# A row-wise softmax in 12 tiles instead of 11: five rows first, nine and six last, and a first store that no longer waits for the third load

## The chip, the core and the metric

The kernel runs on one core of one Trainium2 chip. The core has 16 DMA engines that move data between its on-chip memory (SBUF, 128 partitions) and device memory (HBM), and compute engines that each follow their own queue of instructions. Here four of those queues matter: VectorE (DVE), ScalarE (ACT), GpSimd (POOL) and SyncE (SP). SP, POOL and ACT also issue the transfers. The metric is the time of one execution in microseconds on the device; lower is better. Before the change the median of three runs is 317.19 us (317.1 to 317.5).

## The reference

A softmax over the last axis of a float32 array of 32 x 512 x 1024, after a division by a temperature of 0.5:

```python
def reference(x, temperature):
    scaled = x / temperature
    shifted = scaled - np.max(scaled, axis=-1, keepdims=True)
    exp_x = np.exp(shifted)
    return (exp_x / np.sum(exp_x, axis=-1, keepdims=True)).astype(np.float32)
```

That is 16,384 rows of 1,024 elements, 4 KB each: 67.11 MB are read and as many written, and every element is touched by one maximum, one exponential with a sum, and one multiplication.

## The kernel before

The 16,384 rows are cut into tiles. A tile has 128 partitions, and each partition holds k consecutive rows of the input, so a "tile of twelve rows" is 128 x 12 rows and 6,144 KB. The list `PASSES` (line 10) names the tiles and, inside each tile, the groups of rows that are computed together: one tile of 4+4+4 rows, nine of 6+6 and one of 4+4, 128 rows per partition in all, 11 tiles and 23 groups.

The pool of tiles has four buffers of twelve rows (`BUFS`, line 11). All arithmetic is in place: a tile is loaded, normalised where it lies, and stored from there. The four first loads are issued at once on SP's queue. After that `load()` (line 56) is called once after each store, so the load of tile i+4 stands behind the landing of the store of tile i, whose buffer it takes. SP issues all loads in order.

For each group g there are four steps. `maximum(g)` is one DVE reduction over the group (line 69) and a small DVE multiplication that makes the bias (line 72). `exponential(g)` is one ACT instruction for each row, with the row's sum accumulated beside it (line 78). `divide(g)` takes a reciprocal on DVE (line 90) and multiplies: in tiles listed in `WHOLE` with one tensor-by-tensor multiplication for the whole group (line 93), in the others with one tensor-by-scalar multiplication per row (line 96). `store(g)` issues the store of the whole tile once its last group has been divided (line 108), on POOL's queue for tiles before number `BY_POOL`, on ACT's for the others.

The order on every engine is written out by hand (`manual_schedule`). In a step of the loop, the maximum and exponential of group g come first, and then the division of group g-1, so DVE can reduce the next group while ACT works on the one before. It follows that the store of tile i stands on DVE behind the first reduction of tile i+1, and so behind the landing of load i+1. From tile `ALONE` on the order is turned round at the first group of a tile: the former tile is divided and stored before the next one is reduced.

Ahead of the first store POOL copies one element of tile 2 (line 106). The copy does no work for the result; it makes POOL wait until load 2 has landed before it issues the store of tile 0.

Of the kernel before, what the change touches and what calls it, by code (L numbers as in the profile page):

```python
# [1 line left out]

# [4 lines left out]

PASSES = [[4, 4, 4]] + [[6, 6]] * 9 + [[4, 4]]  # L10
BUFS = 4

WHOLE = (2, 3, 4, 6, 8)


BY_POOL = 6

ALONE = 9


@with_exitstack
def kernel(
    ctx: ExitStack,
    tc: tile.TileContext,
    x: bass.AP,
    temperature: bass.AP,
    out: bass.AP,
):
    nc = tc.nc
    f32 = mybir.dt.float32  # L30
    scale = 1.0 / float(temperature)
    extreme = mybir.AluOpType.max if scale > 0 else mybir.AluOpType.min

    P = 128
    xf = x.flatten_outer_dims()
    of = out.flatten_outer_dims()
    n, d = xf.shape
    rows = [sum(ks) for ks in PASSES]
    assert sum(rows) * P == n

    data = ctx.enter_context(tc.tile_pool(name="data", bufs=BUFS))
    stats = ctx.enter_context(tc.tile_pool(name="stats", bufs=4))


    groups = []
    for i, ks in enumerate(PASSES):
        for j, k in enumerate(ks):
            groups.append((i, sum(ks[:j]), k))

    def dram(t, i):  # L50
        block = t[P * sum(rows[:i]) : P * sum(rows[: i + 1]), :]
        return block.rearrange("(p k) d -> p k d", p=P, k=rows[i])

    tiles, small = [], []

    def load():
        i = len(tiles)
        if i < len(PASSES):
            xt = data.tile([P, rows[i], d], f32, name="xt")
            nc.sync.dma_start(out=xt, in_=dram(xf, i))  # L60
            tiles.append(xt)

    def maximum(g):
        i, a, k = groups[g]
        top, bias, sums, recip = (
            stats.tile([P, k], f32, name=name) for name in ("top", "bias", "sums", "recip")
        )
        small.append((bias, sums, recip))
        nc.vector.tensor_reduce(  # L69
            out=top, in_=tiles[i][:, a : a + k, :], axis=mybir.AxisListType.X, op=extreme  # L70
        )
        nc.vector.tensor_scalar_mul(bias, in0=top, scalar1=-scale)  # L72

    def exponential(g):
        i, a, k = groups[g]
        bias, sums, _ = small[g]
        for b in range(k):
            nc.scalar.activation(  # L78
                tiles[i][:, a + b, :],
                tiles[i][:, a + b, :],  # L80
                mybir.ActivationFunctionType.Exp,
                bias=bias[:, b : b + 1],
                scale=scale,
                accum_out=sums[:, b : b + 1],
            )

    def divide(g):
        i, a, k = groups[g]
        _, sums, recip = small[g]
        nc.vector.reciprocal(recip, sums)  # L90
        if i in WHOLE:
            xt = tiles[i][:, a : a + k, :]
            nc.vector.tensor_mul(xt, xt, recip.unsqueeze(2).to_broadcast([P, k, d]))  # L93
            return
        for b in range(k):
            nc.vector.tensor_scalar_mul(  # L96
                tiles[i][:, a + b, :], in0=tiles[i][:, a + b, :], scalar1=recip[:, b : b + 1]
            )

    def store(g):  # L100
        i, a, k = groups[g]
        if a + k == rows[i]:
            if i == 0:


                nc.gpsimd.tensor_copy(stats.tile([P, 1], f32, name="seen"), tiles[2][:, 0, 0:1])  # L106
            queue = nc.gpsimd if i < BY_POOL else nc.scalar
            queue.dma_start(out=dram(of, i), in_=tiles[i])  # L108
            load()

    with tc.manual_schedule():
        for _ in range(BUFS):
            load()
        for g in range(len(groups) + 1):

            alone = g < len(groups) and groups[g][0] >= ALONE and groups[g][1] == 0
            if g > 0 and alone:
                divide(g - 1)  # L120
                store(g - 1)
            if g < len(groups):
                maximum(g)
                exponential(g)
            if g > 0 and not alone:
                divide(g - 1)
                store(g - 1)


# [1 line left out]
_INS = ['x', 'temperature']  # L131
_OUTS = [((32, 512, 1024), 'float32')]

_NUMBERS = {'temperature': 0.5}


# [26 lines left out]
```

## Time and profile before

| What | Value |
| --- | --- |
| Median of three runs | 317.19 us (317.1 to 317.5) |
| Span of the profiled execution | 315.8 us, so 1.4 us of the median lie outside the span |
| DVE busy / ACT busy / POOL busy | 256.9 us (81%) / 148.3 us (47%) / 3.7 us (1%) |
| Bytes moved, mean rate over the span | 134.24 MB, 425 GB/s |
| First reduction on DVE starts | 18.25 us |
| First store issued by POOL | 47.89 us |
| Last store issued by ACT | 301.35 us |

The page gives the profiled execution's span and no other time of its own; the runs' times stand beside it. Times in the profile count from the start of the span. A line of the timeline reads: start, duration, engine, line of the kernel, operation, what is written and read with its shape, how many, and in brackets how long the engine was idle before it and what ended that. In the row called DMA, each digit is the share of a slice (a fortieth of the span) in which the 16 DMA engines were busy, in tenths. A transfer of a tile is cut into one packet for each partition, eight for each DMA engine; the packet records of the trace give each packet's queue, start, duration and size.

### The profile page before, as it was taken

To read this page: it belongs to the slowest core of one execution; us is meant where nothing else is said; L and a number is where in the kernel's file an instruction comes from. 1 tells how busy PE (TensorE), PEld (TensorE's weight loads), DVE (VectorE), ACT (ScalarE), POOL (GpSimd) and SP (SyncE) were. 2 spreads that over 40 slices of the span, in tenths; PEclk is the share of its full clock that TensorE was granted. 3 is DMA by queue.
4 is the path that set the end of the run, shared out by engine and by line. 5 is a ranking of instruction groups with operands and counts; after the bars stand their busy time and mean duration, and the time that the engine had idled before them with its cause. 6 is when DMAs were issued, how large, how long until landed. Compare 5 with 4: busy or idle time off the path is not lost.

```text
span 315.8 us, 525 instructions
## 1 busy us (share of the span) xinstructions
DVE 256.9 (81%) x147; ACT 148.3 (47%) x257; POOL 3.7 (1%) x11
## 2 busy tenths in 40 slices
DVE  0069999999999899979976994999199999969710
ACT  0029636775461807344471744074416802953700
POOL 0000001000000000000000000000000000000000
DMA  8999999999999999999999999999999999999996
GB/s 305 473 417 423 461 411 399 399 468 430 400 479 417 417 461 411 430 467 405 442 448 399 455 442 405 467 424 417 461 417 430 455 401 463 411 452 411 455 411 270
DMA packets 3171, 134.24 MB, mean 425 GB/s; under 512 B 352, under 2 KB 352, under 8 KB 352
## 3 DMA queue, kind: packets, MB, share of 16 engines
q1 hardware_dynamic: 1584, 67.11, 49.7%
q0 software_dynamic: 864, 37.75, 27.6%
q10 hardware_dynamic: 720, 29.36, 21.5%
q14 instruction: 3, 0.02, 0.0%
HBM read 67.11 MB, written 67.11 MB: 425 GB/s over the span
## 4 chain that ended last, share of the span: by engine, by line
DMA 47%; DVE 28%; ACT 11%; issue 9%; DVEq 0%; SPq 0%; POOLq 0%
DMA xt<-in_x_dram 25%; DMA out_dram<-xt 22%; DVE top L69 16%; ACT xt L78 11%; DVE xt L96 8%; DVE xt L93 2%; DVE bias L72 0%; DVE recip L90 0%; DVEq L158 0%; SPq L60 0%; POOLq L108 0%
## 5 line engine op out<-in xcount | busy, mean ns | idle before, releaser
L78 ACT ACTIVATE xt<-xt,bias 128x1024 f32<-128x1024 f32 x128 | 145.2, 1135 | 131.7 <-DVE recip L90 70.6
L69 DVE TENSOR_REDUCE top<-xt 128x6 f32<-128x6144 f32 (+1 forms) x23 | 139.9, 6083 | 37.8 <-DMA xt<-in_x_dram 37.8
L93 DVE TENSOR_TENSOR xt<-xt,recip 128x6144 f32<-128x6144 f32 x10 | 65.6, 6558 | 0.4
L96 DVE TENSOR_SCALAR xt<-xt,recip 128x1024 f32<-128x1024 f32 x68 | 46.2, 749 | 0.5
L78 ACT ACTIVATION_READ_ACCUMULATOR xt<-xt,bias 128x1 f32 x128 | 23.9, 187 | 0.0
L78 ACT ACT_TABLE_LOAD x1 | 1.3, 1283 | 18.3 <-DMA xt<-in_x_dram 18.3
L90 DVE RECIPROCAL recip<-sums 128x6 f32<-128x6 f32 (+1 forms) x23 | 4.2, 182 | 5.0 <-ACT xt L78 5.0
L108 POOL DMA_DIRECT2D out_dram<-xt x6 | 3.3, 554 | 129.6 <-ACT xt L78 82.7
L72 DVE TENSOR_SCALAR bias<-top 128x6 f32<-128x6 f32 (+1 forms) x23 | 3.9, 171 | 0.8
L106 POOL COPY seen<-xt 128x1 f32<-128x1 f32 x1 | 0.2, 185 | 46.9 <-DMA xt<-in_x_dram 46.9
L144 POOL MEMSET const-uint8-127<- 128x1 uint8 x1 | 0.1, 103 | 0.0
L144 POOL MEMSET const-bfloat16-1.0<- 128x1 bf16 x1 | 0.1, 102 | 0.0
L144 POOL MEMSET const-float32-0.0<- 128x1 f32 x1 | 0.1, 99 | 0.2 <-issue 0.2
L144 POOL MEMSET const-float32-1.0<- 128x1 f32 x1 | 0.1, 98 | 0.0
## 6 DMA issues: line engine op xcount, KB each, us to landing
xt<-in_x_dram SPq DMA_DIRECT2D x10, 6144.0 KB, 36.4
out_dram<-xt POOLq DMA_DIRECT2D x6, 6144.0 KB, 35.9
out_dram<-xt ACTq DMA_DIRECT2D x4, 6144.0 KB, 31.9
xt<-in_x_dram SPq DMA_DIRECT2D x1, 4096.0 KB, 34.9
out_dram<-xt ACTq DMA_DIRECT2D x1, 4096.0 KB, 13.5
```

The lines of the kernel that those rows point to most:

```text
L69: nc.vector.tensor_reduce(out=top, in_=tiles[i][:, a : a + k, :], axis=mybir.AxisListType.X, op=extreme)
L72: nc.vector.tensor_scalar_mul(bias, in0=top, scalar1=-scale)
L78: nc.scalar.activation(tiles[i][:, a + b, :], tiles[i][:, a + b, :], mybir.ActivationFunctionType.Exp, bias=bias[:, b : b + 1], scale=scal ...
L90: nc.vector.reciprocal(recip, sums)
L93: nc.vector.tensor_mul(xt, xt, recip.unsqueeze(2).to_broadcast([P, k, d]))
L96: nc.vector.tensor_scalar_mul(tiles[i][:, a + b, :], in0=tiles[i][:, a + b, :], scalar1=recip[:, b : b + 1])
L106: nc.gpsimd.tensor_copy(stats.tile([P, 1], f32, name="seen"), tiles[2][:, 0, 0:1])
L108: queue.dma_start(out=dram(of, i), in_=tiles[i])
L144: nc = _bacc.Bacc("TRN2", target_bir_lowering=False, num_devices=1)
```

## The change

The tiles become one of 3+2 rows, nine of 6+6, one of 5+4 and one of 3+3: still 128 rows per partition, but 12 tiles and 24 groups. The numbers of the tiles listed in `WHOLE` go up by one each, and so does `ALONE`. POOL issues the stores of tiles 0 to 7, ACT those of tiles 8 to 11. The one-element copy on POOL is gone, so POOL's first store waits for nothing but the data of tile 0.

```diff
-PASSES = [[4, 4, 4]] + [[6, 6]] * 9 + [[4, 4]]
+PASSES = [[3, 2]] + [[6, 6]] * 9 + [[5, 4]] + [[3, 3]]
 BUFS = 4

-WHOLE = (2, 3, 4, 6, 8)
+WHOLE = (3, 4, 5, 7, 9)

-BY_POOL = 6
+BY_POOL = 8

-ALONE = 9
+ALONE = 10
...
     def store(g):
         i, a, k = groups[g]
         if a + k == rows[i]:
-            if i == 0:
-
-
-                nc.gpsimd.tensor_copy(stats.tile([P, 1], f32, name="seen"), tiles[2][:, 0, 0:1])
             queue = nc.gpsimd if i < BY_POOL else nc.scalar
             queue.dma_start(out=dram(of, i), in_=tiles[i])
             load()
```

## The prediction

> **What bounds the kernel now.** I read the page's engine and DMA rows first, then stretches of time by their DMA share, then the waits, last the timeline around the first and last stores. The page:
>
> ```profile
> span 315.8 us, 525 instructions
> ...
> DVE 256.9 (81%) x147; ACT 148.3 (47%) x257; POOL 3.7 (1%) x11
> ...
> DMA  8999999999999999999999999999999999999996
> ...
> q1 hardware_dynamic: 1584, 67.11, 49.7%
> q0 software_dynamic: 864, 37.75, 27.6%
> q10 hardware_dynamic: 720, 29.36, 21.5%
> ```
>
> DVE is busy 81% of the time, but the DMA row is full from the second slice to the last but one. The three queues (SP's loads, POOL's stores, ACT's stores) sum to 98.8% of 16 engines' span, 312.0 us of 315.8. The stretches (start:end, length, busy DVE, ACT, POOL, clock, DMA share, GB/s):
>
> ```profile
> 4.80:49.00 44.20, 30.33 (x24) 19.47 (x32) 0.85 (x2) 1.00 0.99 430
> 49.00:55.00 6.00, 5.93 (x5) 3.32 (x7) 0.00 (x0) 1.00 1.05 385
> 55.00:281.00 226.00, 202.17 (x101) 116.38 (x204) 2.66 (x5) 1.00 1.00 433
> 281.00:303.00 22.00, 18.42 (x20) 9.16 (x16) 0.00 (x0) 1.00 0.99 429
> ```
>
> The rate is 430 with loads alone, 433 mixed, 429 with stores alone: one queue suffices to fill the engines, and who issues makes no difference. The packet records agree: a 49,152-byte packet (one partition of a twelve-row tile) lasts 1,815 ns at the median on all three queues, a 32,768-byte one 1,213 ns. The waits show that compute waits for transfers, and SP for stores:
>
> ```profile
> DVE top L69 <- DMA xt<-in_x_dram: 37.8, 6, 18.2
> ```
> ```profile
> SPq L60 <- DMA out_dram<-xt: 241.2, 7, 74.3
> ```
>
> These waits cost nothing while either ring (the queue of loads, or that of stores) has packets left. The packets sum, for each engine, to (10 x 1.815 + 1.213) x 8 x 2 = 309.81 us. Around that lie: 1.76 us before the first packet; 1.97 us for each engine by which packets last longer than the median, nearly all in two places (0.83 in each engine's first packet, 0.94 in the load packets at 49.6 to 54.4 us, as the first store opens); some 0.2 us of completion packets; and the last engine's lag. The engines' last packets end between 312.83 and 314.53 us, 313.4 in the mean: the slowest is 1.1 us behind. A further 1.2 us end the span. So only some 3 us are neither bytes nor fixed ends. The question for the change is whether its packets cost more, and whether both rings are ever empty together.
>
> **The change part by part.** The sum is made against the profiled span of 315.8; 1.4 us outside it make the median's 317.2, and I keep them.
>
> *Twelve tiles, not eleven.* The bytes stay. 1.815 and 1.213 us differ by 0.602 for 16,384 bytes, so a packet is 0.009 us plus bytes at 27.2 bytes a ns. Packets of 9, 6 and 5 rows (36,864, 24,576, 20,480 bytes) then take 1.364, 0.912 and 0.762 us. The new sum is (9 x 1.815 + 1.364 + 0.912 + 0.762) x 16 = 309.96: +0.14, and +0.02 for two more rounds of completions. **+0.16 us**, all on the path, since the engines are the path.
>
> A rule speaks against more transfers: the Trainium skill's page "DMA: Bandwidth & Descriptors" (section on the anatomy of one DMA) gives a DMA some 2.0 us fixed. As an estimate by it, two more would add 4.0 us where nothing covers them, giving 321.2. The trace has the cover: packets of the next store follow the last one's within one slot, so I take the 0.16.
>
> *First tile of five rows.* It lands at 1.76 + 8 x 0.762 + 1.6 (the slowest engine's start, from load 0 ending 17.88 instead of 1.76 + 14.52) = 9.5 us instead of 17.9. DVE and ACT start 8.4 us sooner, which by itself is worth nothing: they wait for loads afterwards.
>
> *Store 0 without line 106.* The copy ran at 47.31 and DVE's division ended at 47.44, so the copy held nothing back. POOL's rows:
>
> ```profile
> 47.31 0.18 POOL L106 COPY seen<-xt 128x1 f32<-128x1 f32 x1 [46.86 <-DMA xt<-in_x_dram]
> 47.89 0.67 POOL L108 DMA_DIRECT2D out_dram<-xt  x1 [0.40 <-DVE xt L96]
> 69.47 0.53 POOL L108 DMA_DIRECT2D out_dram<-xt  x1 [20.91 <-DVE xt L96]
> 96.49 0.53 POOL L108 DMA_DIRECT2D out_dram<-xt  x1 [26.49 <-ACT xt L78]
> ```
>
> Now the division of tile 0's second group stands on DVE behind the first reduction of tile 1. Load 1 lands at 9.5 + 14.5 = 24.0; reduction from 24.3. From one reduction to the next the timeline shows 9.52 us where four rows are divided by line 96 (37.83 to 47.35) and 10.86 where six are (58.21 to 69.07). With two rows: 8.15, so the next reduction starts at 32.5, and POOL issues store 0 at 32.9 (47.89 was 0.45 after such an end). It first moves data 4.0 to 4.4 us after its issue if it repeats 47.89 to about 52: at 37. The loads in the ring then reach to 1.76 + 0.83 + 41 rows (6.1 + 3 x 14.5) = 52 us, so nothing runs dry here.
>
> *The hand-over at 58 us, the thinnest place.* In a mean engine loads 0 to 2 end at 1.76 + 0.83 + 6.09 + 29.04 + 0.94 = 38.7. Packets of the two rings alternate, one for one (so they do in the records after 55 us). Load 3 and store 0 share: load 3 ends at 38.7 + 14.5 + 6.1 = 59.3, store 0 at 57.5 or a load packet sooner. Load 4 can be issued once store 0 has landed on all engines: 57.9, and SP's 0.44 (76.76 to 77.20) make 58.3; its data come 1.0 us later (0.74 to 1.76) at best, 4.2 (77.20 to 81.40) behind a busy ring: 59.3 to 62.5. Store 1: reductions at 32.5, 43.3 and 54.2, the division of tile 1 ends there, POOL issues at 54.6, data from 58.6 to 59.0, or 60.7 if it takes the 6.1 us that the mean engine's first store packet took in all. Against 59.3 that is between no gap and 1.4 us. I take **none**: the later figure counts the load packet that was under way, and here none is queued any more. The end of the range keeps the 1.4.
>
> *The nine tiles of twelve.* After that place each store is issued before the former has ended. Store 2: reductions at 54.2, 65, division done by 76, issued 76.5; store 1 ends about 59 + 14.5 + 6 load packets x 1.8 = 85. 8.5 us in hand; in the trace of before store 4 was issued at 153.74 and could move at 161, 7.4 in hand. The period stays 16 x 1.815 = 29.0 us a tile, DVE needs 2 x 13.4 = 26.9 in a `WHOLE` tile and 21.7 in the others. Cost **0**, hidden by the ring of stores; if it fails, each late store costs what exceeds its 7 to 8 us.
>
> *Stores 6 and 7 from ACT to POOL; tiles 2, 6 and 8 by line 96, 5, 7 and 9 by line 93.* Packets cost the same from both. ACT loses two issues of 0.34 us that it had time for; POOL has 1% of its time used. Still five tiles go by line 93, each 5 us longer on DVE than one by line 96; they only change places, inside the 29.0 us that each tile has. **0**.
> The Trainium skill's page "SBUF — State Buffer" (the "DVE blocks DMA" trap) speaks against it: POOL can't write descriptors while DVE runs a two-port operation, which tensor-by-scalar in fp32 may be. In the trace line 96 ran from 159.98, 6.2 us after the store issued at 153.74, and that store moved data as soon as the former left the ring (about 161). By the rule a store could wait for one group, 4.1 us, still within the time in hand.
>
> *Tail.* At 38.7 us 29 rows have been read and none stored; that lead, 29 x 1.21 = 35 us, less some 3 in which stores run alone (59 to 62), is what stores still need when the last load (six rows) has ended: it lands 32 us before the end. Then reduce 3.4, three exponentials 3.6, the second group's 3.4 and a division 2.3, with small ones 13.5 us, and 1.9 to move: ready 15 to 17 us after landing. The last store's own packets need 7.3, so 6 to 9 us are in hand; before, it was issued at 301.35 and the ring freed at 303.1. **0**. The slowest engine's lag, 1.1 us now, is made of chance delays in single packets: kept, with 0.6 either way.
>
> Sum: +0.16. Span 315.9, time **317.4**, no difference that can be told: within 0.2% (0.63 us) is what a measurement of this kernel cannot tell from no change.
>
> **The rivals.**
> - *Slower: the rings run dry at 58 us.* One mechanism: store 1, held on DVE behind tile 2's reduction, has not reached the engines when load 3 ends, and load 4 is still behind store 0's landing. It decides from the point where store 1 moves data later than 59.8 us, and costs up to 1.4: 317.8 to 318.8, 318.3 in the middle. For it: margins of 0.3 to 0.7 us. Against: load 4 arrives at nearly the same time, and the leading engines' idle time is not the slowest's.
> - *Slower: POOL's two extra stores, or DVE's order, make a store late in the bulk.* More than 8 us of lateness would be needed; each us beyond it costs one. 318.5 to 320. Nothing in the rows speaks for it.
> - *Faster: the two one-time delays shrink with the packets.* 0.83 x 7/12 = 0.48 from the first packets and 0.94 x 7/12 = 0.55 from the first store's: 317.35 - 1.03 = 316.3, or 316.8 if one of them does. For it: 20 KB packets stand there now. Against: around 52 us packets on all engines are delayed, those begun at 50.0 as those begun at 51.5, which looks like an event of a fixed length.
> - *The removed wait does nothing.* True by the rows above; it is part of the forecast.
>
> **How the numbers follow.** Forecast 0.60; dry rings 0.15 (a third of it stays within 0.63 us); late stores in the bulk 0.06; shrinking delays 0.16 (a small part stays within); chance in the last engine's lag splits the last 0.03. Faster 0.16, same 0.64, slower 0.20. The range: low end 316.4, where both delays shrink; high end 318.6, forecast and most of the dry gap; outside it lie the late stores and the extremes, under 2 in 10.
>
> **What would show it.** Reduction at about 9.8 us; store 0 issued near 33 and store 1 near 54.6; DMA share 1.0 and 433 GB/s from 62 to 280 us; POOL's issues 7 to 10 us before the former store ends; the last issue by ACT 5 us or more before its first packet. A slice of the DMA row below 9 around 58 to 62 us would show the slower rival, a rate near 430 at 32 to 40 us the faster one. A stretch at much less than 433 in the bulk would show that the rate depends on who issues, and make the whole prediction wrong.

## The result, and the profile after

The changed kernel takes 318.58 us (median of 22 runs, 318.17 to 319.88), the kernel before 317.25 us beside it. The ratio, taken over the single runs and so not the quotient of the two medians, is 1.0033 with a 95% interval of 1.002 to 1.0046. The forecast was no difference (317.4 us); what came is slower by 1.3 us, 0.02 us inside the upper end of the stated range. Runs over 1.5% above the fastest of the same kernel count as a slower state and are left out of every median, range and ratio here (two runs each of two kernels below).

The page of the changed kernel, the rows that answer to those shown before:

```profile
span 316.8 us, 536 instructions
...
DVE 257.5 (81%) x150; ACT 148.5 (47%) x257; POOL 4.6 (1%) x12
...
DMA  7999999999999999999999999999999999999996
...
q1 hardware_dynamic: 1728, 67.11, 49.7%
q0 software_dynamic: 1152, 46.66, 34.0%
q10 hardware_dynamic: 576, 20.45, 15.0%
```

The transfers are still the bound: the DMA row is full from the second slice to the last but one, and the three queues sum to 98.7% of the 16 engines' span, 312.7 us against 312.0. Compute has not become it: DVE grew by 0.6 us. The stretches of time (start:end, length, busy DVE, ACT, POOL, clock, DMA share, GB/s):

```profile
4.80:32.00 27.20, 15.58 (x12) 7.77 (x12) 0.00 (x0) 1.00 1.01 439
32.00:40.00 8.00, 7.93 (x6) 6.72 (x13) 0.67 (x1) 1.00 0.93 334
...
56.00:64.00 8.00, 7.93 (x8) 4.03 (x9) 0.00 (x0) 1.00 0.99 427
64.00:250.00 186.00, 162.52 (x81) 91.46 (x160) 3.20 (x6) 1.00 1.00 434
250.00:281.00 31.00, 29.69 (x10) 14.57 (x27) 0.00 (x0) 1.00 1.01 429
```

The bulk runs at 434 GB/s, as before. Two stretches look slower than they should be. One is 32 to 40 us, where the first store opens (334); but the stretch beside it makes up for that, and from 4.80 to 64 us the rate is 428 against 426 before. The other is 250 to 281 us at 429, where the kernel before had this line:

```profile
250.00:281.00 31.00, 27.75 (x16) 16.76 (x30) 0.00 (x0) 1.00 1.01 437
```

The packet records show what happens there. I took from each packet's time the time its size should take (0.009 us and 27.2 bytes a ns); what is left is its delay. The records do not name the 16 engines, so I followed each one by joining a packet to the one that ended as it began. Where two engines change packets at the same moment this cannot tell them apart; the means over 16 engines do not depend on it.

```
us, of one profile each             before    changed
packets, by size                    310.01    310.17
delays, mean of 16 engines            1.97      2.61
  in the first packets                0.83      0.62
  as the first store opens            0.99      1.29
  from 255 to 285 us                  0.01      0.59
mean engine ends                    313.39    314.21
last engine ends                    314.53    315.63
span                                315.75    316.84
```

So the mean engine ends 0.82 us later, of which 0.16 is packets and most of the rest delays, and the last engine lags by 1.42 instead of 1.14. Together that is 1.1 us of span. Each run's time is 1.7 to 1.8 us above its span; the profiled run of before was one of 317.5 us, 0.25 above its median, which is the rest of the 1.33. (The 1.4 us outside the span that stand ahead of the prediction set that run's span against the median of three; against the run's own time it is 1.7.)

The last engine matters because all 16 have the same 192 data packets to move, eight of each transfer. In the changed kernel seven engines end at 315.1 to 315.6 and nine at 313.0 to 313.9. Two things go with a late engine there. First, one engine, the one whose first packet ended latest, is delayed in two load packets as the first store opens (1.06 and 0.69 us; the other fifteen lose 0.8 to 1.3 in one of them, and up to 0.4 in another). Its first store packet moves at 40.38, theirs between 38.66 and 39.50. I call such an engine, whose first store packet comes well after those of the others, a straggler. It ends at 315.36, among the late ones but not last. Second, of the eight engines that took ACT's first packet before POOL's last one, seven are delayed by 0.6 to 1.6 us between 258 and 280 us and one by 0.3; the other eight by 0.0 to 0.2. In the kernel before, the first store packets move between 52.26 and 55.00 without a straggler; the five engines whose first store packet moves earliest, four of them the latest after their first packet, get the smaller delay (0.4 to 1.0 in sum, the others 0.9 to 1.5), and every engine finishes POOL's packets before ACT's first.

### The profile page after: what moved, and what is told of

The parts are those of the page before. It is cut to its first block, busy times and chain, and to the rows that moved or that the text cites. A ratio compares the mean times of both kernels' runs of the same rounds, so it can differ in the third digit from the quotient of the medians.

```text
span 316.8 us, 536 instructions
## 1 busy us (share of the span) xinstructions
DVE 257.5 (81%) x150; ACT 148.5 (47%) x257; POOL 4.6 (1%) x12
## 4 chain that ended last, share of the span: by engine, by line
DMA 62%; issue 14%; DVE 13%; ACT 6%; POOL 0%; DVEq 0%; SPq 0%; POOLq 0%
DMA xt<-in_x_dram 39%; DMA out_dram<-xt 23%; DVE top L69 9%; ACT xt L78 6%; DVE xt L96 3%; DVE recip L90 0%; POOL out_dram L104 0%; DVEq L154 0%; DVE bias L72 0%; SPq L60 0%; POOLq L104 0%
## 5 line engine op out<-in xcount | busy, mean ns | idle before, releaser
L69 DVE TENSOR_REDUCE top<-xt 128x6 f32<-128x6144 f32 (+4 forms) x24 | 140.1, 5837 | 39.0 <-DMA xt<-in_x_dram 39.0
L90 DVE RECIPROCAL recip<-sums 128x6 f32<-128x6 f32 (+4 forms) x24 | 4.4, 182 | 5.0 <-ACT xt L78 4.9
L104 POOL DMA_DIRECT2D out_dram<-xt x8 | 4.4, 550 | 219.3 <-ACT xt L78 118.8
L72 DVE TENSOR_SCALAR bias<-top 128x6 f32<-128x6 f32 (+4 forms) x24 | 4.1, 171 | 0.8
```

The source lines that it names most:

```text
L69: nc.vector.tensor_reduce(out=top, in_=tiles[i][:, a : a + k, :], axis=mybir.AxisListType.X, op=extreme)
```

## The experiments

Each time is a median; the ratio is to the kernel before on the same chip, over the single runs, with its 95% interval. What is said of packets comes from one profiled execution of each kernel. Delays "of 255 to 285 us" are the mean of the 16 engines in that stretch, as in the table.

### The changed kernel once more

Edit: none.

> The changed kernel once more. Its first profile has an end 1.1 us later than before: 0.16 us of packets, some 0.6 us more in delayed packets (mean of 16 engines), and a last engine that lags more. Seven of the 16 engines are delayed by 0.2 to 0.7 us a packet between 258 and 280 us, where ACT's stores begin while POOL's last one still runs. Theory A (the place is fixed: the switch of queues delays these packets): the same delays at 258 to 280 us, ratio 1.003 to 1.0045. Theory B (the opening: the first store after 33 us delays load packets by 1.29 us instead of 0.94): the delays at 258 to 280 are chance and are gone or elsewhere, the opening's stay near 1.3, ratio the same. Theory C (chance in one profile): neither is seen again.

Measured: 318.51 us, ratio 1.0017 (0.9997 to 1.0037); the median beside it is 317.51, and runs of before scatter up to 320.9 in this set, which widens the interval. The ratio lies under the 1.003 that theories A and B gave; the interval holds it. The opening's delay is there again (1.37 us in the mean) and so is the single straggler (0.95 and 1.05 us; first store packet at 40.76, the others by 39.57; it ends at 315.15, the last engine at 315.54). The delays of 255 to 285 us are there too, but fewer: four engines with 0.6 to 1.1 us, 0.24 in the mean. All four had ACT's first packet before POOL's last; two more engines with that order have none. Theory C falls.

### All stores on POOL

```diff
-BY_POOL = 8
+BY_POOL = 12
```

> The changed kernel with all twelve stores on POOL, so there is no switch of queues at all. Theory A: the delays at 258 to 280 us go, and most of the loss with them: ratio to the kernel before 1.0005 to 1.0015 (the 0.16 us of packets and a little). Theory B: no change against the changed kernel, 1.003 to 1.0045.

Measured: 318.48 us, 1.0013 (0.9989 to 1.0036). The time is that of the changed kernel, 318.51 in the same set. But the delays of 255 to 285 us are gone (0.01), as theory A said:

```profile
281.00:303.00 22.00, 17.87 (x23) 11.77 (x22) 1.07 (x2) 1.00 0.99 430
303.00:313.00 10.00, 0.00 (x0) 0.00 (x0) 0.00 (x0) 1.00 0.98 421
```

The mean engine ends at 313.61, 0.22 after before's, as 0.16 of packets allow. Other things keep the time up. The straggler of the opening (1.29 and 0.49 us; first store packet at 40.70, the others by 39.44) ends at 315.09, the next one at 314.20. And the span ends 1.60 us after the last packet instead of 1.21. Of the 0.94 us by which this span is longer than that of before, 0.56 lie in the last engine's end and 0.38 behind it. Taking away the switch from POOL's queue to ACT's does not bring the time back.

### Only the last store on ACT

```diff
-BY_POOL = 8
+BY_POOL = 11
```

> The changed kernel with stores 0 to 10 on POOL and only the last on ACT. All stores on POOL had no delayed packets after 240 us, but its span ended 1.6 us after the last packet instead of 1.2. If both readings hold: no delays at 258 to 280 us, 1.2 us after the last packet, ratio 1.001 to 1.002. If the switch costs wherever it is: delayed packets in the last 10 us, ratio 1.003.

Measured: 318.48 us, 1.0016 (0.9996 to 1.0036). Delays of 255 to 285 us: 0.13, on three engines, though the switch comes only with the last store, at 305.7 us. The span ends 1.38 us after the last packet. The last two engines end at 315.25 (delays spread over the run) and 315.10 (the straggler: 0.91 and 0.93, first store packet at 40.70 against 39.48). As with all stores on POOL, the time stays.

### The wait for load 2 put back

```diff
+            if i == 0:
+                nc.gpsimd.tensor_copy(stats.tile([P, 1], f32, name="seen"), tiles[2][:, 0, 0:1])
             queue = nc.gpsimd if i < BY_POOL else nc.scalar
```

> The changed kernel with the one-element copy on POOL put back, so the store of the five-row tile waits for load 2 (some 41 us) instead of going out at 33. Theory A: no change, 1.003 to 1.0045. Theory B: the opening's delay falls from 1.3 to some 0.95 us, ratio 1.0015 to 1.003. If the wait protects loads against a dry spell or makes one at 50 to 62 us, a DMA share under 1.0 shows there and the ratio rises by up to 1 us (1.006).

Measured: 319.01 us, 1.0045 (1.002 to 1.0071). The copy made POOL wait this time:

```profile
39.29 0.18 POOL L104 COPY seen<-xt 128x1 f32<-128x1 f32 x1 [38.85 <-DMA xt<-in_x_dram]
39.87 0.79 POOL L106 DMA_DIRECT2D out_dram<-xt  x1 [0.39 <-DVE recip L90]
```

The store goes out at 39.87 instead of 33.07, the opening's delay falls to 0.88 us, as theory B said, and the time doesn't: six runs lie at 318.2 to 318.4 and six at 319.6 to 321.1. The profiled one (320.12) has four engines at 315.6 to 317.1 and twelve by 313.8. So the mean of the opening's delay is not what sets the time; theory B falls in that form. There is no dry spell either (DMA share 0.97 to 1.00 from 40 to 62 us). But the delays of 255 to 285 us are 0.50 here, although POOL's last data packet began on every engine (254.2 at the latest) before ACT's first one on any (255.7).

### Five rows late instead of first

```diff
-PASSES = [[3, 2]] + [[6, 6]] * 9 + [[5, 4]] + [[3, 3]]
+PASSES = [[4, 4, 4]] + [[6, 6]] * 8 + [[3, 2]] + [[5, 4]] + [[3, 3]]
```

> The changed kernel with its tiles in another order: nine of twelve rows first, then five, nine and six, so the same packets and twelve tiles, but the kernel opens as before with a twelve-row tile. Theory A: the opening is as before, the switch of queues is still there (tile 8), ratio 1.0015 to 1.0045 depending on whether ACT's first store still overlaps POOL's last. Theory B: 1.0005 to 1.0015. If only the number of tiles costs: 1.0005.

Measured: 321.53 us, 1.0102 (1.0067 to 1.0137). No theory had this. The end runs dry:

```profile
303.00:313.00 10.00, 5.85 (x10) 4.92 (x10) 0.00 (x0) 1.00 0.67 285
```

The last store is issued at 310.27, after the nine-row store has drained on most engines (by 308.1), and the engines lie idle for 3.1 us in the mean. My reading, not tested: with three small tiles in a row too few stores are left to cover the last tiles' compute. The run says nothing on the opening, but shows the price of empty rings, which the prediction's first rival put at another place.

### All stores on ACT, changed kernel and before

```diff
-BY_POOL = 8
+BY_POOL = 0
```

> The changed kernel with all twelve stores on ACT, none on POOL: no switch of queues. The delay of load packets as the first store opens (1.27 to 1.37 us a packet in the runs with POOL) either goes, if it belongs to POOL's descriptors, or stays near 1.0 to 1.3, if it belongs to the first writes. Theory A (the switch): no delayed packets after 240 us, last engine under 314.8, ratio 1.0 to 1.002. Theory B (the opening): the ratio stays 1.003 if the opening's delay stays, and falls to about 0.999 if it goes. ACT then waits for each division before it takes the next exponentials; DVE waits at most 0 to 2 us for that, which the transfers hide.

```diff
-BY_POOL = 6
+BY_POOL = 0
```

> The kernel before with all stores on ACT; the twin of the changed kernel with all stores on ACT. Whatever the opening costs there with and without POOL must show here too: the delay of load packets at the first store (0.94 us a packet) goes if it is POOL's, stays if it is the first writes'. Ratio 0.997 to 0.998 if it goes; 0.999 to 1.001 if it stays. The rival that ACT's waits now hold up exponentials: the last store is issued later than 302 us and the DMA share falls before the end, 1.002 and more.

Measured: changed 318.30 us, 1.0039 (1.0001 to 1.0078), with runs from 317.49 to 321.91; before 317.87 us, 0.9999 (0.9976 to 1.0022). The opening's delay stays without POOL, 1.44 and 1.16 us against 1.29 and 0.99 with it. So it belongs to the opening of the stores, not to POOL's descriptors. In before's twin two engines are stragglers (first store packets at 53.9, the others by 53.25); they end last, at 314.7. In the changed one the profiled run is one of 321.7: fifteen engines end by 315.5, one at 318.78, with some 4 us of delays after the opening that are not tied to any place. Theory A misses here: there is no switch of queues at all, yet the delays of 255 to 285 us are 0.47 in the mean, on six engines. So such delays do not need the switch.

### The kernel before with POOL issuing eight stores

```diff
-BY_POOL = 6
+BY_POOL = 8
```

> The kernel before with POOL issuing stores 0 to 7, nothing else changed, so that ACT's first store (tile 8, issued at some 260 us) opens while POOL's store of tile 7 runs to some 271 us. Theory A: some engines take ACT's first packet ahead of POOL's last, and these are delayed by 0.6 to 1.6 us after that; ratio 1.002 to 1.005. Theory B: no change, 0.999 to 1.001.

Measured: 317.79 us, 1.0007 (0.9981 to 1.0033). Here all 16 engines take ACT's first packet before POOL's last, and fifteen of them have no or small delays (up to 0.2 us), one 0.6. The profile (318.47) loses time otherwise: the engines lie idle for 1.65 us in the mean between 300 and 310 us, before the last store. Theory A's rule that this order itself delays an engine falls.

### The first store a little later

```diff
+            if i == 0:
+                nc.gpsimd.tensor_copy(stats.tile([P, 768], f32, name="seen"), tiles[0][:, rows[0] - 1, 0:768])
             queue = nc.gpsimd if i < BY_POOL else nc.scalar
```

That is the larger shift; the smaller copies one element.

> The changed kernel; POOL copies one element of the finished tile 0 before it issues the first store, so the store goes out some 0.2 to 0.5 us later (33.3 to 33.6 instead of 33.07) and nothing else moves. In every profile of the changed kernel one DMA engine that started late is delayed in two load packets as the first store opens (1.75 to 2.0 us in sum, the others 1.0 to 1.3 in one packet), stays 1.2 to 2 us behind and ends last. Theory E (the place of the first store in the rhythm of packets, 1.8 us long, decides who is delayed twice): at a shift this small the late engine is still hit twice, ratio 1.003 to 1.0045. Theory B (the opening costs whatever its place): the same.

> The same with a copy of 768 elements, so the first store goes out some 0.9 to 1.3 us later (34.0 to 34.4). Theory E: the late engine's packet ends before the delay begins, it is hit once, its sum falls under 1.5 us and the last engine ends at 314.0 to 314.8 instead of 315.5; ratio 1.0005 to 1.0025. Theory B: no change, 1.003 to 1.0045.

Measured: 319.35 us, 1.0062 (1.0042 to 1.0081) with one element and 318.80 us, 1.0047 (1.0033 to 1.0061) with 768; both ratios are above what theory E gave. POOL's rows of the larger shift:

```profile
33.18 0.82 POOL L104 COPY seen<-xt 128x768 f32<-128x768 f32 x1 [32.73 <-DVE xt L96]
33.94 0.67 POOL L106 DMA_DIRECT2D out_dram<-xt  x1
```

The store goes out 0.87 us later than in the changed kernel. With the smaller shift (33.25) the straggler is as before: 0.72 and 1.36 us, first store packet at 41.00 against 39.44 at most, and it ends at 316.02, here as the last engine. (The expectation says that it had ended last in every profile. Of the changed kernel's two and those with eleven and all stores on POOL that is so only in the last; in the others it ended among the late ones.) With the larger one no engine is hit like that: no sum is over 1.6 us, and the first store packets spread from 38.59 to 40.62 without a gap at the end. That is what theory E said of the packets. The time does not follow, nor the last engine's end: twelve engines end by 313.75, the earliest at 312.82, but four at 314.4 to 315.2, and these four are the ones that took ACT's first packet before POOL's last.

### Five rows second

```diff
-PASSES = [[3, 2]] + [[6, 6]] * 9 + [[5, 4]] + [[3, 3]]
+PASSES = [[6, 6]] + [[3, 2]] + [[6, 6]] * 8 + [[5, 4]] + [[3, 3]]
```

> The changed kernel with the five-row tile second and a twelve-row tile first; everything from the third tile on is the same. Theory F (the small first packets make one engine start later than it would): the latest engine is under 0.7 us behind the median after its first packet, as before, and the ratio is 1.0005 to 1.002. Theory E: it depends on where the first store falls; anything from 1.0005 to 1.004, together with a late engine hit twice where it is high. If only the number of tiles or the tail costs: 1.003 to 1.0045 with no engine hit twice.

Measured: 318.94 us, 1.0035 (1.0001 to 1.0068), from 317.48 to 320.39. Theory F falls on its packets: the latest engine is 1.4 us behind the median after its first packet, not under 0.7, though that packet is of a twelve-row tile. Its time is missed too, but the interval is wide. Two of the seven runs are at 317.5. Twelve tiles with this tail can thus be run within 0.1 us of before's median beside them (317.43), so neither the number of tiles nor the tail needs to cost 1.3 us. The profiled run (320.12) has fourteen engines by 314.0, one at 314.9 and one at 317.1.

### The first store of the kernel before 0.9 us later

```diff
-                nc.gpsimd.tensor_copy(stats.tile([P, 1], f32, name="seen"), tiles[2][:, 0, 0:1])
+                nc.gpsimd.tensor_copy(stats.tile([P, 768], f32, name="seen"), tiles[0][:, rows[0] - 1, 0:768])
```

> The kernel before; the one-element copy of tile 2 is replaced by a copy of 768 elements of the finished tile 0, so the first store goes out some 0.7 to 1.2 us later (48.6 to 49.1 instead of 47.89). In the profile of before the engines that were late got the smaller delay (0.4 to 0.7 us, the others 0.9 to 1.5) and caught up. Theory E: that order is lost, the late engines are hit as hard as the others or harder, the last one ends 0.4 to 1.2 us later; ratio 1.001 to 1.004. Theory B: no change, 0.999 to 1.001.

Measured: 319.08 us, 1.0044 (1.002 to 1.0067). POOL's rows:

```profile
48.03 0.82 POOL L106 COPY seen<-xt 128x768 f32<-128x768 f32 x1 [47.59 <-DVE xt L96]
48.80 0.66 POOL L108 DMA_DIRECT2D out_dram<-xt  x1
```

In the kernel before, nine tenths of a microsecond on one store cost as much as the whole change. The packets show theory E's part: two stragglers (first store packets at 55.94 and 56.28, the others by 55.08; the last one delayed by 0.57 and 1.04), which end at 314.63 and 315.55 while the other fourteen end by 314.22. They show a second part that E did not have. The last store is issued later, and the engines lie idle for 0.62 us in the mean between 300 and 310 us:

```profile
303.47 0.34 ACTq L108 DMA_DIRECT2D out_dram<-xt  x1
```

In the kernel before that issue was at 301.35, and its first packet followed at 303.14 without a gap. So this run mixes two causes, a straggler and a tail that runs dry, and does not tell how much is whose.

## Why the prediction was right or wrong, point by point

**The bound, and the twelve tiles: right.** Packets of 9, 6 and 5 rows take 1.364, 0.912 and 0.761 us, and the sum is 310.17 against 310.01, the +0.16 forecast. Two runs at 317.5 with five rows second fit that this is all that twelve tiles need to cost. The same holds for who issues: all stores on POOL, eight, and none give 318.48, 318.58 and 318.30. The Trainium skill's page "DMA: Bandwidth & Descriptors" (its rules for kernel authors) says that spreading transfers over issuing engines doesn't add bandwidth, and these runs agree. Its fixed 2 us for each transfer did not show as time, and the trap that "SBUF — State Buffer" warns of, POOL's descriptors starved by DVE, did not show as time either with twelve POOL stores.

**First tile and first stores: right.** The first reduction starts at 10.00 (forecast 9.8), POOL's issues are these (forecast 32.9, 54.6, 76.5); the first store's data moved at 38.7, not 37:

```profile
33.07 0.67 POOL L104 DMA_DIRECT2D out_dram<-xt  x1 [32.62 <-DVE xt L96]
54.79 0.53 POOL L104 DMA_DIRECT2D out_dram<-xt  x1 [21.06 <-DVE xt L96]
76.49 0.53 POOL L104 DMA_DIRECT2D out_dram<-xt  x1 [21.17 <-DVE xt L96]
```

**The hand-over at 58 us: right that it costs nothing.** The second store's data move from 59.2, as load 3 ends; the DMA share from 56 to 64 us is 0.99. The slower rival put its loss here, and there is none here. The range's upper end, 318.6, was reckoned from that loss. That the measured 318.58 still lies inside it is luck: another cost filled the place of the one that did not come. Against the forecast itself, 317.4 and no difference beyond 0.63 us, the 1.3 us are a miss, and "slower" had been given 0.20. (Two slips in how those numbers follow: the parts named for "slower" add to 0.16 and at most the 0.03 of chance, and both delays shrinking gives 316.3, not the 316.4 of the range.)

**The bulk: right**, 434 GB/s and no store late.

**The move of stores 6 and 7: right in the sum, wrong in what it left out.** ACT's first store was issued at 249.63 while POOL's last one ran to 259 us, so three queues shared the engines. That held up POOL's last store, whose completion packets came as late as 262.6, and load 11 behind it until 263.07 (259.7 with all stores on POOL). "Packets cost the same from both" holds for the median packet, 1,815 ns on all three queues; the delays of 255 to 285 us fall in this stretch, but whether the move brings them is not shown.

**The tail: 6 to 9 us in hand were forecast, there were 2.4.** Load 11 landed 25 us before the end (290.2 of 315.6), not 32, and the hold-up just told is the larger part: with all stores on POOL the load's data ended 5 us earlier (283.4 instead of 288.4). The last store was issued at 303.48 and its first packet moved at 305.84. It cost nothing, but the margin was not known.

```profile
263.07 0.33 SPq L60 DMA_DIRECT2D xt<-in_x_dram  x1
...
303.48 0.34 ACTq L104 DMA_DIRECT2D out_dram<-xt  x1
```

**The step that failed: the delays, held fixed, and with them the lag.** The prediction kept the two one-time delays at 0.83 and 0.94 and put nothing for delays elsewhere; of the rest it wrote "The slowest engine's lag, 1.1 us now, is made of chance delays in single packets: kept, with 0.6 either way". Measured were 0.62 and 1.29, another 0.59 from 255 to 285 us, and a lag of 1.42. So the delays grew from 1.97 to 2.61, almost all of that late in the run, and with 0.16 of packets the mean engine ended 0.82 later; the lag added 0.28, inside its own 0.6. Together that is 1.1 us at the last engine. Nor does the lag look like chance alone: a straggler at the first store stands in the changed kernel's two profiles and in three of its variants, each time the engine whose first packet ended latest, and it ends between 315.1 and 316.0 each time. The faster rival was wrong on the same step: the first packets' delay did shrink (by 0.21), but the store's grew (by 0.30) with smaller store packets.

**What is shown and what stays open.** Shown, for the profiled executions: the loss is in delayed packets and in when the last of 16 engines ends; more packets are 0.16 us of it, and the bulk's rate, compute and an empty ring are none of it. Shown as well: no single one of the parts tried brings the time back. Without the switch from POOL to ACT the straggler remains (all stores on POOL, and eleven); without the straggler late engines remain (larger shift); both times the time stays where it was. What makes the engines late is not shown. The switch alone cannot be it: delays of 255 to 285 us of the same size come with no switch (all stores on ACT, 0.47) and with no data packet of ACT's ahead of POOL's last (the wait put back, 0.50), and hardly any with all engines in that order (the kernel before with eight stores on POOL, 0.05). With the smaller shift four engines that had finished POOL's packets first were delayed by 0.6 to 0.9 us. Being out of step is not enough either: the stragglers with all stores on POOL and with eleven are not delayed there. So the cause stays open. Not tried: all stores on POOL together with the larger shift, which has neither switch nor straggler.

## What to carry to other kernels

Where the DMA engines are full from end to end, the time is set by the last one of 16, and the mean rate no longer tells kernels apart: compare when each engine's packets end. What puts one engine behind costs its whole lag, and here removing one suspected cause changed nothing. In the kernel before, a shift of one early store by 0.9 us cost as much as the change of the whole tiling, so a difference of 0.3% says little on the tiling itself.

## What the runs showed that was not expected

- When the first store opens, load packets on every engine are delayed once by about 1 us (0.88 to 1.44 in the mean of 16 engines), on POOL's queue and on ACT's alike, and later stores show nothing like it.
- The two rings alternate packet for packet whatever the sizes, as the prediction had reckoned; less expected is how long that makes a small store: eight 20,480-byte store packets went one for one with 49,152-byte load packets, so the five-row store took from 38.7 to 57.3 us, most of it the loads' time.
- The spread from run to run differs at the same bytes and tiles. The changed kernel's 22 runs lie within 1.7 us, seven with five rows second over 2.9 us (317.48 to 320.39), and ten with all stores on ACT over 4.4 us (317.49 to 321.91).
